# FFN projections as three 256-column matmuls per weight tile, with the two parts of their inputs in separate blocks

## The chip, the cores and the metric

The kernel runs on one core of a Trainium2 chip. The metric is the device time of one execution in microseconds. The engines are TensorE (PE; its weight loads are PEld), VectorE (DVE), ScalarE (ACT), GpSimd (POOL) and SyncE (SP). On-chip memory (SBUF) has 128 partitions; addresses below are bytes within a partition. Matmuls write to banks of PSUM.

## The reference

The input is a sequence of 256 tokens of width 1024, in float32. Two layers follow each other; a layer is

```
x = x + 0.5 * swiglu_ffn(rms_norm(x, ffn1_norm), gate_up, down)
x = x + mixer(rms_norm(x, mix_norm))       # layer 0: convolutions; layer 1: dilated attention
x = x + 0.5 * swiglu_ffn(rms_norm(x, ffn2_norm), gate_up, down)
```

where `swiglu_ffn(x) = (silu(gate) * up) @ w_down` with `gate, up = split(x @ w_gate_up)` and a hidden width of 2816. A last RMS norm ends it. There are therefore four FFN stages (two in each layer), and each multiplies 256 tokens by 1024 x 5632 and by 2816 x 1024 weights.

## The kernel before

Activations lie transposed: 128 features on the partitions, 256 tokens along the row. All weights come as one stream of "units" of 128 x 2048 floats (1 MB), which is 16 weight tiles of 128 x 128; SyncE's queue loads them in order into four `raw` buffers. For most units ScalarE then makes a rounded copy `w1` in the format fp32r (L126) and VectorE the remainder `w2 = raw - w1` (L127); `advance` (L130) issues loads and splits a few units ahead of their use. The unit buffers lie at multiples of 1024 bytes, so a weight tile of 512 bytes starts at 0 or at 512 modulo 1024.

Activations are split into two parts in the same way: the first part rounded, the second the remainder (`split_to`, L183). A product is then w1 x first + w1 x second + w2 x first; w2 x second is left out. There are two ways to write it:

- `mm3` (L158): three matmuls of 256 columns for a weight tile, L162 with w1 and the first part, L163 with w1 and the second, L164 with w2 and the first, all into the same 256 columns of PSUM.
- `mm2` (L166): two matmuls, L168 with w1 and both parts side by side as 512 columns, L169 with w2 and the first part as 256 columns. It leaves two halves in PSUM that are yet to be added.

An FFN stage (`ffn`, L364) has 22 projection steps of one unit each: a gate block and an up block of 128 features, 8 tiles each. With `project` (L314, mm3) gate and up fill one PSUM bank; with `project2` (L324, mm2) they fill two, and `join` (L334) adds the halves: a ScalarE copy (L338), a VectorE add (L339) for each, then a multiply by the norm's factor r (L340). Behind it come silu (L385), the product (L387) and the split into `gs` (L186, L187). `ONES` and `ONE_END` say which steps use mm3: the first 4, 0, 0 and 2 of the four stages, and the last one. Then come 8 output blocks of 22 tiles each (11 units): mm2 for seven of them, mm3 for the last, each added into x at L404 (once for each PSUM half). The mixers use mm3 (and plain fp32 matmuls, L160, for some units), but for the queries and keys of the attention, which use `project2`.

Each FFN or mixer reads its input from `xs`, which `Norm.add` (L287) fills block by block as the stage before it finishes. `xs` and `gs` hold, for each block of 128 features, the first part (1024 bytes) and behind it the second. Where they start is set by `XS_START` and `GS_START`; the tile `xs` itself is at a multiple of 1024, and the tile `gs` lies at 256 modulo 1024 in the first three stages and at 320 in the last.

TensorE executes its instructions in program order; the framework orders them by the program and its priorities, so that the first steps of a stage may stand among the last matmuls of the stage before.

Of the kernel before, what the change touches and what calls it, by code (L numbers as in the profile page):

```python
# [11 lines left out]
F32R = mybir.dt.float32r  # L12
# [5 lines left out]
P = 128  # L18
D = 1024
S = 256  # L20
DEPTH = 2
FF = 2816
ND = D // P
NF = FF // P
# [27 lines left out]
ONES = [4, 0, 0, 2]  # L52
ONE_END = 1
PRIO_F = 0
FFN_STEP = 40
# [4 lines left out]
WIDEC = 0  # L60
LINE = 1024
BASE = 16512
XS_START = {"F1": (288, 32), "MX": (192, 256), "F2": (288, 32)}
GS_START = (800, 800, 800, 736)
GROUPS = ((0, 2), (2, 4), (4, 6), (6, 8))
M_POOL = [0, 0, 0, 0]
B_POOL = [0, 0]
# [10 lines left out]
C_F1, C_MX, C_F2, C_FN = 0, DEPTH * ND, 2 * DEPTH * ND, 3 * DEPTH * ND  # L78
# [15 lines left out]
def trunk(ctx: ExitStack, tc: tile.TileContext, xin, wst, cst, bia, idn, out):  # L94
    nc = tc.nc
    keep = ctx.enter_context(tc.tile_pool(name="keep", bufs=1))
# [12 lines left out]
    at = {"load": 0, "split": 0}  # L109
# [20 lines left out]
    def advance(u, ahead_split=ahead_split):  # L130
        while at["load"] < min(n_units, u + ahead_load):
            load(at["load"])
            at["load"] += 1
        while at["split"] < min(n_units, u + ahead_split):
            split(at["split"])
            at["split"] += 1
# [3 lines left out]
    whole = {0} | {first_conv + i for i in WHOLE}  # L140

    class Stream:
        def __init__(self, u):
            self.u = u
# [8 lines left out]
    def take(n):  # L153
        st = Stream(used[0])
        used[0] += n
        return st

    def mm3(o, a, b, start, stop, check=False):  # L158
        if len(a) == 1:
            nc.tensor.matmul(o, a[0], b[-1], start=start, stop=stop, skip_group_check=check)  # L160
            return
        nc.tensor.matmul(o, a[0], b[0], start=start, stop=False, skip_group_check=check)  # L162
        nc.tensor.matmul(o, a[0], b[1], start=False, stop=False, skip_group_check=check)  # L163
        nc.tensor.matmul(o, a[1], b[0], start=False, stop=stop, skip_group_check=check)  # L164

    def mm2(o, w, b, start, stop):  # L166

        nc.tensor.matmul(o, w[0], b, start=start, stop=False, skip_group_check=True)  # L168
        nc.tensor.matmul(o[:, 0], w[1], b[:, 0], start=False, stop=stop, skip_group_check=True)  # L169


    x = keep.tile([P, ND, S], F32, name="x")
    xs_all = keep.tile([P, ND * 2 * S + LINE // 4], F32R, name="xs")
    const_all = keep.tile([P, LINE // 4], F32, name="const")
    const = const_all[:, :NCONST]
    ident = keep.tile([P, P], F32, name="ident")
# [6 lines left out]
    def split_to(o1, o2, src, scale=None):  # L183

        if scale is None:
            nc.scalar.copy(o1, src)  # L186
            nc.vector.tensor_sub(o2, src, o1.bitcast(F32))  # L187
        else:
            nc.scalar.activation(o1, src, AF.Copy, scale=scale)  # L189
            nc.vector.scalar_tensor_tensor(o2, src, scale, o1.bitcast(F32),  # L190
                                           op0=ALU.mult, op1=ALU.subtract)
# [86 lines left out]
    class Norm:  # L278


        def __init__(self, col, whole=None, start=0):
            self.col, self.whole = col, whole
            self.xs = xs_all[:, start // 4:start // 4 + ND * 2 * S].rearrange(
                "p (d t s) -> p d t s", d=ND, t=2)
            self.sums = tmp.tile([P, S], F32, name="sums")

        def add(self, d):  # L287
# [23 lines left out]
    def twice(r):  # L311
        return r[:, None, :].to_broadcast([P, 2, S])

    def project(st, base, xs, xg=None):  # L314

        bank = psa.tile([P, 2, S], F32, name="pa")
        for i in range(2):
            for k in range(ND):
                w = st.tile(base + 2 * k + i)
                b = (xs[:, k, 0], xs[:, k, 1]) if len(w) == 2 else (xg[:, k],)  # L320
                mm3(bank[:, i], w, b, k == 0, k == ND - 1)
        return bank

    def project2(st, base, xs):  # L324

        banks = []
        for i in range(2):
            bank = psa.tile([P, 2, S], F32, name="pa")
            for k in range(ND):
                mm2(bank, st.tile(base + 2 * k + i), xs[:, k], k == 0, k == ND - 1)  # L330
            banks.append(bank)
        return banks

    def join(v, banks, r):  # L334

        for i, bank in enumerate(banks):
            h = tmp.tile([P, S], F32, name="sq")
            nc.scalar.copy(h, bank[:, 1])  # L338
            nc.vector.tensor_add(v[:, i], bank[:, 0], h)  # L339
        nc.vector.tensor_mul(v, v, twice(r))  # L340
# [23 lines left out]
    def ffn(norm, after, between=None, first=None):  # L364
        _, r = norm.end(True, first is None)
        with tc.tile_pool(name="gp", bufs=1, reuse_waits="tile") as gp:
            st = take(NF)
            start = GS_START[st.u // FFN_STEP] // 4
            gs = gp.tile([P, NF * 2 * S + start], F32R, name="gs")[:, start:].rearrange(
                "p (f t s) -> p f t s", f=NF, t=2)  # L370
            for p in range(NF):
                advance(st.u + p)
                one = p < ONES[st.u // FFN_STEP] or p >= NF - ONE_END
                if one:
                    bank = first if first and p == 0 else project(st, p * UT, norm.xs)
                else:
                    banks = project2(st, p * UT, norm.xs)
                with tc.high_priority(offset=PRIO_F):
                    v = tmp.tile([P, 2, S], F32, name="v")
                    if one:  # L380
                        nc.vector.tensor_mul(v, bank, twice(r))
                    else:
                        join(v, banks, r)
                    sl = tmp.tile([P, S], F32, name="sl")
                    nc.scalar.activation(sl, v[:, 0], AF.Silu)  # L385
                    g = tmp.tile([P, S], F32, name="g")
                    nc.vector.tensor_mul(g, sl, v[:, 1])  # L387
                    split_to(gs[:, p, 0], gs[:, p, 1], g)
            if between:
                between(gs[:, NF - 1, 0, :1].bitcast(F32))  # L390
            st = take(NF * ND // UT)
            for d in range(ND):
                acc = psb.tile([P, 2, S], F32, name="pb")
                two = d < ND - 1
                for f in range(NF):
                    t = d * NF + f
                    if t % UT == 0 or f == 0:
                        advance(st.u + t // UT)
                    if two:
                        mm2(acc, st.tile(t), gs[:, f], f == 0, f == NF - 1)  # L400
                    else:
                        mm3(acc[:, 0], st.tile(t), (gs[:, f, 0], gs[:, f, 1]), f == 0, f == NF - 1)
                for i in range(2 if two else 1):
                    nc.vector.scalar_tensor_tensor(x[:, d], acc[:, i], 0.5, x[:, d],  # L404
                                                   op0=ALU.mult, op1=ALU.add)
                after.add(d)

    def out_half(st, accs, half, o, ds, ahead=(ahead_split,) * 2):

        for d in ds:  # L410
            for k in range(4):
                t = half * 32 + d * 4 + k
                if t % UT == 0:
                    advance(st.u + t // UT, ahead[t // UT % 2])
                mm3(accs[d // 2][:, d % 2], st.tile(t), [a[:, k] for a in o],
                    half == 0 and k == 0 and d % 2 == 0, half == 1 and k == 3, True)
# [290 lines left out]
    cold = psb.tile([P, P], F32, name="pb")  # L707
    for _ in range(WARM):
        nc.tensor.matmul(cold, ones, ones, start=True, stop=True)
    norm = Norm(C_F1, start=XS_START["F1"][0])  # L710
    for layer in range(DEPTH):
        nxt = Norm(C_MX + layer * ND, start=XS_START["MX"][layer])
        if layer == 0:
            ffn_first(norm, nxt)
        else:
            ffn(norm, nxt)
        norm, nxt = nxt, Norm(C_F2 + layer * ND, start=XS_START["F2"][layer])
        (conv if layer % 2 == 0 else attention)(norm, nxt)
        if layer < DEPTH - 1:
            norm, nxt = nxt, Norm(C_F1 + (layer + 1) * ND, start=XS_START["F1"][layer + 1])  # L720
            ffn(norm, nxt)
            norm = nxt
    with tc.tile_pool(name="fp", bufs=1, reuse_waits="tile") as fp:
# [7 lines left out]
        for i, (lo, hi) in enumerate(GROUPS):  # L731
            n = hi - lo
# [93 lines left out]
```

## Time and profile before

| | |
|---|---|
| time, median of 2 runs | 960.42 us (959.98 to 960.87) |
| the profiled execution's own time | 960.66 us |
| its span, first to last instruction | 958.9 us |
| PE busy | 945.5 us (99%), 5828 matmuls |
| weight loads busy | 845.8 us, 5828 loads |
| VectorE busy | 724.3 us (76%) |
| ScalarE busy | 543.3 us (57%) |
| granted clock of TensorE, mean | 0.997 |
| memory traffic | 176.24 MB, 184 GB/s |

A share of busy time is the union of an engine's instructions. Matmuls overlap in the pipeline, so the step of a stream of them is read from the starts, and not from the length of one.

### The profile page before, as it was taken

Reading aid. Unit: us, or ns where it says so; the run is one execution under the profiler, and the core shown is the slowest. Engines: PE = TensorE matmul, PEld = TensorE weight load, DVE = VectorE, ACT = ScalarE, POOL = GpSimd, SP = SyncE. Lnnn points to the kernel's source line nnn. Section 1 sums busy time; section 2 is a strip of 40 time slices with the busy share of each in tenths; the row PEclk is TensorE's granted clock in tenths of the full one; section 3 lists DMA queues with packets and bytes.
Section 4 is the critical chain, followed back from the end, with each engine's and each line's share of the span. In section 5 each row is a group of like instructions: output and inputs, shape, how many; then the busy total and the mean of one; then the engine's idle time right before and its main releaser. Section 6 shows DMA issues by size and latency. Waiting matters only on the chain.

```text
span 958.9 us, 15090 instructions
## 1 busy us (share of the span) xinstructions
PE 945.5 (99%) x5828; PEld 845.8 (88%) x5828; DVE 724.3 (76%) x1373; ACT 543.3 (57%) x975; POOL 47.1 (5%) x61
## 2 busy tenths in 40 slices
PE   8999999999999999999999999999999999999996
PEld 7988898999888888988988889898888998889886
DVE  7988866688879878766788877665698798788552
ACT  6666554488265565554466565444676565665541
POOL 0000000049600000000000000000000000000000
PEclk9999999999999999999999999999999999999998
DMA  8855555544176555555455555555553455555501
GB/s 328 291 205 192 178 206 189 178 159 148 45 260 213 193 207 181 180 211 181 176 194 202 176 191 205 178 195 212 195 191 129 149 186 194 194 202 177 194 26 44
DMA packets 27287, 176.24 MB, mean 184 GB/s; under 512 B 3024, under 2 KB 3792, under 8 KB 6864
## 3 DMA queue, kind: packets, MB, share of 16 engines
q1 hardware_dynamic: 26784, 174.67, 51.7%
q8 instruction: 45, 0.74, 0.3%
q10 hardware_dynamic: 432, 0.63, 0.2%
q14 instruction: 26, 0.21, 0.1%
HBM read 174.23 MB, written 1.05 MB: 183 GB/s over the span
## 4 chain that ended last, share of the span: by engine, by line
PE 90%; POOL 3%; DVE 3%; ACT 1%; DMA 1%; issue 1%; SPq 0%; DVEq 0%; POOLq 0%; ACTq 0%
PE pa L168 33%; PE pa L169 17%; PE pb L168 15%; PE pb L169 8%; PE pa L162 4%; PE pa L163 3%; PE pa L164 3%; POOL yp L486 3%; PE pa L160 2%; PE pb L162 1%; PE pb L163 1%; PE pb L164 1%; DVE pb L463 1%; PE pa L352 1%; PE pb L652 1%
## 5 line engine op out<-in xcount | busy, mean ns | idle before, releaser
L127 DVE TENSOR_TENSOR w<-raw,w 128x1024 fp32r<-128x1024 f32 (+1 forms) x316 | 377.0, 1205 | 136.3 <-ACT w L126 135.9
L168 PE MATMUL pa<-xs,w 128*128 128x512 f32 x1376 | 479.4, 391 | 0.1
L126 ACT CAST w<-raw 128x1024 fp32r<-128x1024 f32 (+1 forms) x316 | 320.5, 1032 | 133.5 <-PE pa L168 49.7
L169 PE MATMUL pa<-xs,w 128*128 128x256 f32 x1376 | 387.2, 282 | 0.0
L168 PEld LDWEIGHTS pa<-xs,w 128*128 128x128 f32 x1376 | 258.1, 188 | 54.9 <-DVE xs L190 0.7
L169 PEld LDWEIGHTS pa<-xs,w 128*128 128x128 f32 x1376 | 260.0, 189 | 0.3
L168 PE MATMUL pb<-gs,w 128*128 128x512 f32 x616 | 213.7, 390 | 0.0
L169 PE MATMUL pb<-gs,w 128*128 128x256 f32 x616 | 173.7, 282 | 0.0
L168 PEld LDWEIGHTS pb<-gs,w 128*128 128x128 f32 x616 | 115.6, 188 | 24.1
L169 PEld LDWEIGHTS pb<-gs,w 128*128 128x128 f32 x616 | 116.4, 189 | 0.0
L385 ACT ACTIVATE sl<-v 128x256 f32<-128x256 f32 x88 | 36.8, 418 | 108.7 <-DVE v L340 104.3
L338 ACT COPY sq<-pa 128x256 f32<-128x256 f32 x172 | 62.9, 366 | 28.6 <-PE pa L169 26.1
L163 PE MATMUL pa<-xs,w 128*128 128x256 f32 x272 | 76.3, 281 | 0.1
L162 PE MATMUL pa<-xs,w 128*128 128x256 f32 x272 | 76.3, 282 | 0.0
L164 PE MATMUL pa<-xs,w 128*128 128x256 f32 x272 | 76.2, 281 | 0.0
L339 DVE TENSOR_TENSOR v<-pa,sq 128x256 f32<-128x256 f32 x156 | 65.5, 420 | 0.0
L404 DVE SCALAR_TENSOR_TENSOR x<-pb,x 128x256 f32<-128x256 f32 x60 | 25.4, 423 | 42.5 <-PE pb L169 28.5
L189 ACT ACTIVATE xs<-x,const 128x256 fp32r<-128x256 f32 x48 | 24.3, 506 | 55.2 <-DVE x L404 43.1
L486 POOL TENSOR_TENSOR yp<-yp,prod 128x256 f32<-128x256 f32 x55 | 45.1, 822 | 208.8 <-ACT prod L485 204.8
L340 DVE TENSOR_TENSOR v<-v,rr 128x512 f32<-128x512 f32 x78 | 53.6, 688 | 0.0
L162 PEld LDWEIGHTS pa<-xs,w 128*128 128x128 f32 x272 | 51.4, 190 | 0.3
L163 PEld LDWEIGHTS pa<-xs,w 128*128 128x128 f32 x272 | 51.1, 188 | 0.5 <-DVE xs L190 0.3
(155 smaller groups left out, 900.7 us busy)
## 6 DMA issues: line engine op xcount, KB each, us to landing
raw<-wst SPq DMA_DIRECT2D x159, 1024.0 KB, 4.8
bt<-bia SPq DMA_DIRECT2D x8, 384.0 KB, 3.3
raw<-wst SPq DMA_DIRECT2D x7, 256.0 KB, 6.3
raw<-wst SPq DMA_DIRECT2D x2, 512.0 KB, 5.6
x<-xin SPq DMA_DIRECT2D x3, 256.0 KB, 5.7
out<-y SPq DMA_DIRECT2D x2, 256.0 KB, 2.5
out<-y ACTq DMA_DIRECT2D x2, 256.0 KB, 2.4
x<-xin SPq DMA_DIRECT2D x2, 128.0 KB, 3.2
```

Of the source, the lines that this page charges most:

```text
L126: nc.scalar.copy(w1[u][:, c], raw[u][:, c])
L127: nc.vector.tensor_sub(w2[u][:, c], raw[u][:, c], w1[u][:, c].bitcast(F32))
L162: nc.tensor.matmul(o, a[0], b[0], start=start, stop=False, skip_group_check=check)
L163: nc.tensor.matmul(o, a[0], b[1], start=False, stop=False, skip_group_check=check)
L164: nc.tensor.matmul(o, a[1], b[0], start=False, stop=stop, skip_group_check=check)
L168: nc.tensor.matmul(o, w[0], b, start=start, stop=False, skip_group_check=True)
L169: nc.tensor.matmul(o[:, 0], w[1], b[:, 0], start=False, stop=stop, skip_group_check=True)
L338: nc.scalar.copy(h, bank[:, 1])
L339: nc.vector.tensor_add(v[:, i], bank[:, 0], h)
L340: nc.vector.tensor_mul(v, v, twice(r))
L385: nc.scalar.activation(sl, v[:, 0], AF.Silu)
L486: nc.gpsimd.tensor_add(yp[:, c], yp[:, c], t)
```

## The change

All FFN tiles are multiplied with `mm3`. The new function `blocks` lays the inputs out as two blocks: all first parts together, and all second parts together behind them, each block with a start of its own modulo 1024 bytes. `XS_AT` and `GS_AT` give these two starts for each stage, `GS_BASE` the place modulo 1024 that the tile `gs` itself has. For the mixers' inputs (`MX`) both starts stay what they were, 192 and 256. The tile `xs` grows by 2048 bytes.

```
-XS_START = {"F1": (288, 32), "MX": (192, 256), "F2": (288, 32)}
-GS_START = (800, 800, 800, 736)
+XS_AT = {'F1': ((192, 256), (128, 128)), 'MX': ((192, 192), (256, 256)), 'F2': ((192, 320), (448, 448))}
+GS_AT = ((192, 448), (64, 128), (320, 320), (384, 384))
+GS_BASE = (256, 256, 256, 320)
+THREE = (0, 1, 2, 3)
...
+    def blocks(t, base, at, n):
+        lo = (at[0] - base) % LINE
+        step = n * S * 4 + (at[1] - at[0]) % LINE
+        a = t[:, lo // 4:(lo + 2 * step) // 4].rearrange("p (t q) -> p t q", t=2)
+        return a[:, :, :n * S].rearrange("p t (k s) -> p k t s", k=n)
...
-    xs_all = keep.tile([P, ND * 2 * S + LINE // 4], F32R, name="xs")
+    xs_all = keep.tile([P, ND * 2 * S + 3 * LINE // 4], F32R, name="xs")
...
-        def __init__(self, col, whole=None, start=0):
+        def __init__(self, col, whole=None, at=(0, 0)):
             self.col, self.whole = col, whole
-            self.xs = xs_all[:, start // 4:start // 4 + ND * 2 * S].rearrange(
-                "p (d t s) -> p d t s", d=ND, t=2)
+            self.xs = blocks(xs_all, 0, at, ND)
...
-            start = GS_START[st.u // FFN_STEP] // 4
-            gs = gp.tile([P, NF * 2 * S + start], F32R, name="gs")[:, start:].rearrange(
-                "p (f t s) -> p f t s", f=NF, t=2)
+            n = st.u // FFN_STEP
+            gs = blocks(gp.tile([P, NF * 2 * S + 3 * LINE // 4], F32R, name="gs"), GS_BASE[n],
+                        GS_AT[n], NF)
             for p in range(NF):
                 advance(st.u + p)
-                one = p < ONES[st.u // FFN_STEP] or p >= NF - ONE_END
+                one = n in THREE or p < ONES[n] or p >= NF - ONE_END
...
-                two = d < ND - 1
+                two = d < ND - 1 and n not in THREE
...
-    norm = Norm(C_F1, start=XS_START["F1"][0])
+    norm = Norm(C_F1, at=XS_AT["F1"][0])
```

The other calls of `Norm` take `at=XS_AT[...]` in the same way.

## Rows read from the trace of the kernel before

**Rows 1.** The page: span, and busy time, share and instructions of each engine.
```profile
span 958.9 us, 15090 instructions
...
PE 945.5 (99%) x5828; PEld 845.8 (88%) x5828; DVE 724.3 (76%) x1373; ACT 543.3 (57%) x975; POOL 47.1 (5%) x61
```

**Rows 2.** The page: the chain of work that ended last, by engine.
```profile
PE 90%; POOL 3%; DVE 3%; ACT 1%; DMA 1%; issue 1%; SPq 0%; DVEq 0%; POOLq 0%; ACTq 0%
```

**Rows 3.** Two stretches: length, busy PE, PEld, DVE, ACT, POOL; PEclk, DMA share, GB/s.
```profile
31.40:125.60 94.20, 94.20 (x545) 83.51 (x544) 78.91 (x126) 58.72 (x105) 0.00 (x0) 1.00 0.60 212
...
131.30:184.60 53.30, 53.30 (x309) 47.25 (x308) 34.42 (x48) 25.71 (x35) 0.00 (x0) 1.00 0.54 196
```

**Rows 4.** Waits of PE, the longest: total us, times, longest us.
```profile
PE pa L352 <- DVE xg L348: 1.9, 1, 1.9
```

**Rows 5.** Timeline of PE (start, length): first and last L168 of two stretches.
```profile
31.43 0.40 PE L168 MATMUL pa<-xs,w 128*128 128x512 f32 x1
...
125.39 0.39 PE L168 MATMUL pa<-xs,w 128*128 128x512 f32 x1
...
131.33 0.39 PE L168 MATMUL pb<-gs,w 128*128 128x512 f32 x1
...
184.37 0.39 PE L168 MATMUL pb<-gs,w 128*128 128x512 f32 x1
```

**Rows 6.** Timeline of PE: first and last tile of one output block.
```profile
184.72 0.28 PE L162 MATMUL pb<-gs,w 128*128 128x256 f32 x1
...
192.07 0.28 PE L162 MATMUL pb<-gs,w 128*128 128x256 f32 x1
```

**Rows 7.** Groups of PE by line: count, busy us, mean ns, idle before.
```profile
L168 PE MATMUL pa<-xs,w 128*128 128x512 f32 x1376 | 479.4, 391 | 0.1
...
L168 PE MATMUL pb<-gs,w 128*128 128x512 f32 x616 | 213.7, 390 | 0.0
...
L162 PE MATMUL pa<-xs,w 128*128 128x256 f32 x272 | 76.3, 282 | 0.0
...
L162 PE MATMUL pb<-gs,w 128*128 128x256 f32 x88 | 24.5, 279 | 0.0
```

**Rows 8.** Timeline of PE in the convolution's input projection: start, and later.
```profile
192.89 0.28 PE L163 MATMUL pa<-xs,w 128*128 128x256 f32 x1
...
194.59 0.28 PE L163 MATMUL pa<-xs,w 128*128 128x256 f32 x1
...
227.33 0.28 PE L163 MATMUL pa<-xs,w 128*128 128x256 f32 x1
...
231.92 0.28 PE L163 MATMUL pa<-xs,w 128*128 128x256 f32 x1
```

**Rows 9.** Timeline of PE in the attention's output projection.
```profile
750.90 0.28 PE L162 MATMUL pa<-o,w 128*128 128x256 f32 x1
...
752.70 0.28 PE L162 MATMUL pa<-o,w 128*128 128x256 f32 x1
```

**Rows 10.** fp32 matmuls of 256 columns: a run of 13 (timeline), their mean (groups).
```profile
277.84 2.97 PE L160 MATMUL pa<-ob,raw 128*128 128x256 f32 x13
...
L160 PE MATMUL pa<-ob,raw 128*128 128x256 f32 x64 | 14.2, 381 | 0.0
```

**Rows 11.** Groups of VectorE and ScalarE around the join, the splits and x.
```profile
L127 DVE TENSOR_TENSOR w<-raw,w 128x1024 fp32r<-128x1024 f32 x304 | 368.4, 1223 | 133.6 <-ACT w L126 133.2
L339 DVE TENSOR_TENSOR v<-pa,sq 128x256 f32<-128x256 f32 x156 | 65.5, 420 | 0.0
...
L404 DVE SCALAR_TENSOR_TENSOR x<-pb,x 128x256 f32<-128x256 f32 x60 | 25.4, 423 | 42.5 <-PE pb L169 28.5 <-PE pb L164 12.7
...
L338 ACT COPY sq<-pa 128x256 f32<-128x256 f32 x172 | 62.9, 366 | 28.6 <-PE pa L169 26.1 <-DVE sq L187 1.1 <-DVE v L339 1.1
```

**Rows 12.** Timeline of PE in a query and key projection of the attention.
```profile
694.73 0.40 PE L168 MATMUL pa<-xs,w 128*128 128x512 f32 x1
...
699.58 0.40 PE L168 MATMUL pa<-xs,w 128*128 128x512 f32 x1
```

More of the change, by code (lines that the diff above doesn't have):

```diff
@@ L709, in trunk @@
         nc.tensor.matmul(cold, ones, ones, start=True, stop=True)
-    norm = Norm(C_F1, start=XS_START["F1"][0])
+    norm = Norm(C_F1, at=XS_AT["F1"][0])
     for layer in range(DEPTH):
-        nxt = Norm(C_MX + layer * ND, start=XS_START["MX"][layer])
+        nxt = Norm(C_MX + layer * ND, at=XS_AT["MX"][layer])
         if layer == 0:
@@ L716, in trunk @@
             ffn(norm, nxt)
-        norm, nxt = nxt, Norm(C_F2 + layer * ND, start=XS_START["F2"][layer])
+        norm, nxt = nxt, Norm(C_F2 + layer * ND, at=XS_AT["F2"][layer])
         (conv if layer % 2 == 0 else attention)(norm, nxt)
         if layer < DEPTH - 1:
-            norm, nxt = nxt, Norm(C_F1 + (layer + 1) * ND, start=XS_START["F1"][layer + 1])
+            norm, nxt = nxt, Norm(C_F1 + (layer + 1) * ND, at=XS_AT["F1"][layer + 1])
             ffn(norm, nxt)
```

## Prediction

> **What bounds the kernel now.** I read the page first. TensorE (PE) is busy for 945.5 of a span of 958.9 us [rows 1], and the chain of work that ended last runs through PE for 90% of the span [rows 2]. Busy is not yet "at its peak", so the next view is the table by stage: in a projection stretch and in a down stretch PE is busy for the whole of the stretch at a granted clock of 1.00, which is the 2.4 GHz level, with weights arriving at 212 and 196 GB/s [rows 3]. The list of waits says the same from the other side: the longest wait of PE anywhere is 1.9 us, at the very start [rows 4]. So inside the feed-forward (FFN) stages the time is the number of weight tiles times the step from one tile to the next on PE, and nothing else.
>
> The step is read from the timeline, first start to last start over the count, because a matmul's own length (282 or 390 ns) overlaps its neighbours'. A two-matmul tile (L168 with 512 columns, then L169 with 256): in a down stretch 154 L168 start from 131.33 to 184.37 us, 153 steps of 346.7 ns; in a projection stretch 272 start from 31.43 to 125.39, 271 steps of 346.7 ns [rows 5]. A three-matmul tile (L162 to L164, 256 columns each): the last output block of the same down stage goes from 184.72 to 192.07 in 21 tiles, 350.0 ns each, 116.67 per matmul [rows 6]. 768 columns at 2.4 GHz would be 320 ns for either form, so both carry 27 to 30 ns a tile that isn't columns.
>
> **The change, part by part.** *Matmuls.* L168 ran 1376 times on xs, of which 128 belong to the attention's queries and keys (8 pairs of 16 tiles) and stay; 616 times on gs [rows 7]. So 1248 + 616 = 1864 tiles go from two matmuls to three: 1864 more matmuls and 1864 more weight loads. At the step of [rows 6], which is the one for the *old* places, that is 1864 x (350.0 - 346.7) = **+6.2 us**, all on the path, since PE has no slack there.
>
> *Places.* This is the unknown. Today both parts of every FFN input start at 32 modulo 256 bytes (288 and 32 for xs; for gs 256 + 800 or 320 + 736, which is 32 modulo 1024); weight tiles start at 0 or 512. The new places are all multiples of 64: modulo 256, xs (192, 0), (192, 64), (128, 128), (192, 192) and gs (192, 192), (64, 128), (64, 64), (128, 128) for the four stages in order. Tiles added or grown are whole multiples of 1024, so nothing else moves within its 1024. What does the trace say of the step at other places? The three-matmul form also runs in the mixers, with the same weights. The convolution has both parts at 192: at its start 5 tiles take 192.89 to 194.59, 340.0 ns each, **113.33** per matmul; later, behind a stall, 13 tiles take 227.33 to 231.92, 353.1 ns, **117.7** [rows 8]. The attention's output projection reads its input at 0 modulo 256: 5 tiles from 750.90 to 752.70, 360.0 ns, **120.0** [rows 9]. So the same instruction costs from 113.3 to 120.0, by its place and by how the stream was entered. Above, 120.0 is the bound. Below, a bound from another form: 13 fp32 matmuls of 256 columns take 2.97 us, less the last one's 0.38 from issue to end, so 215.8 ns a step, 2.5 over twice 106.7 (256 columns at 2.4 GHz) [rows 10]; with the same 2.5 a 256-column fp32r step would be 109.2.
>
> After the change 1864 + 232 tiles of the FFN are three-matmul tiles (the 232: 144 on xs, that is 272 less the convolution's 128, and 88 on gs [rows 7]), 6288 matmuls, so each ns of step is worth 6.3 us: time = 960.66 + 6.2 + 6.288 x (step - 116.67). It gives 919.9 at 109.2, 945.9 at 113.33, 966.9 at 116.67, 973 at 117.7 and 987.8 at 120.0.
>
> I take **114.0**: the new places are on the grid of the convolution's 192, whose stream entered without a stall stood at 113.33, the nearest row; some of the eight stretches will fall into a slower rhythm, as the convolution did, and 80% at 113.33 with 20% at 116.67 makes 114.0. Then 960.66 + 6.2 - 6.288 x 2.67 = **950.1**.
>
> A rule of the Trainium skill speaks against any gain by place. By "TensorE: Matmul & The Clock Gate" (Step-by-step: what each phase is for), the moving operand and the weight load have two independent SBUF read ports, so that a load takes nothing from a running matmul; by it, places would change nothing and the change would only add. The trace disagrees: four steps for one shape, as above.
>
> *Joining the halves.* For 78 pairs of banks the join goes: 156 adds of 420 ns and the same number of 366 ns copies, and the multiply by r now reads PSUM; seven of eight output blocks also lose one of two 423 ns additions into x [rows 11]. All of it lies beside PE, which waits for none of it, so I cost it at nothing; VectorE and ScalarE get freer, not later. The same cover is what would hide it if the step fell: a weight unit of 16 tiles at 109.2 x 48 = 5.2 us still needs only two splits of 1.22 us on VectorE [rows 11] and 1 MB from memory, 200 GB/s where 212 is already seen [rows 3].
>
> *One PSUM bank instead of two per projected block.* PE can run further ahead at a stage's start. The stalls there are single ones within the 13.4 us that PE idles in all [rows 1]; taken at zero, ends -1.5 and +1 us (its longest wait is 1.9 [rows 4]).
>
> *Two blocks.* The attention's 512-column matmul now reads two runs 8 KB apart instead of 1 KB, at an unchanged place. Steady, its tile takes 694.73 to 699.58 in 14 steps, 346.4 ns [rows 12], the same as in the FFN. Taken at zero; if the jump cost as much as a third matmul, 128 x 3.3 ns = 0.4 us.
>
> The profiled execution took 960.66 us, 1.8 us around its span, and is 0.2 us above the median of 960.42, so the sum stands for the median too.
>
> **Rivals.** *Places don't matter* (the rule above): every stretch stays at 116.67 as [rows 6], **967 us**. For it: places 288 and 32 don't differ now, and two-matmul tiles are 346.7 in both kinds of stretch. Against it: [rows 8, 9]. Chance 0.15.
>
> *Conflict-free places*: the load and the moving read no longer meet, the step falls below 112.6, towards 109.2: **920 to 941 us**, faster by over 2%. For it: the fp32 step shows that 2.5 ns of extra is possible [rows 10], and separate places for the two parts give each matmul of the three its own offset against the weights. Against it: no fp32r row is steady below 113.3. Chance 0.33.
>
> *Worse places*: at 0 modulo 256 the three-matmul step is 120.0; the second part of stage 1's xs is put there, and if 64 and 128 behave like 0 rather than like 192, all is at 120.0: **988 us**. It decides from a mean step of 118.7 on (979.6 us). Against it: only one place of sixteen is 0, and it is read by one matmul of three in one stage's projections. Chance 0.08. Between the two, at the convolution's later 117.7, stands 973 us, chance 0.06.
>
> That the change would miss its places is excluded by the sizes above.
>
> **The numbers.** My forecast, a mean step from 112.6 to 116.0 (941 to 963 us), has 0.38. With 2% (19 us, about what a measurement here can tell from no change) the borders are 941.2 and 979.6: faster 0.33, same 0.38 + 0.15 + 0.06 = 0.59, slower 0.08. The range goes from near the conflict-free end, 922, to 971, which leaves out about 0.07 below (steps under 109.5) and 0.12 above. The forecast's own range is 941 to 963.
>
> **What would show it.** No L168 on gs and 128 on xs left; L162 1248 + 144 + 128 = 1520 on xs and 704 on gs. First start to last start in each of the eight stretches gives its step: about 340 ns a tile where I am right, 350 where places don't matter, 328 where conflicts go. A step that differs between stretches at equal places would say that the entry, not the place, sets it. I am wrong if PE shows idle time inside a stretch, since then a supplier and not the step would bound.

## The result, and the profile after

The changed kernel takes 977.94 us (median of 2 runs, 977.34 to 978.55) against 960.42: 1.0173 times the time before, interval 1.0150 to 1.0196. That is slower by 1.7%, outside the range of 922 to 971 us. The profiled execution took 978.55 us.

The page of the changed kernel: span, busy time of the engines, chain by engine, and groups of instructions, as in [rows 1, 2, 7, 11].

```profile
span 976.8 us, 18444 instructions
...
PE 961.9 (98%) x7692; PEld 936.0 (96%) x7692; DVE 661.0 (68%) x1189; ACT 493.6 (51%) x819; POOL 47.2 (5%) x61
...
PE 91%; POOL 3%; DVE 3%; DMA 1%; ACT 1%; issue 0%; SPq 0%; DVEq 0%; POOLq 0%; ACTq 0%
...
L172 PE MATMUL pa<-xs,w 128*128 128x256 f32 x1520 | 426.2, 281 | 0.0
...
L172 PE MATMUL pb<-gs,w 128*128 128x256 f32 x704 | 197.4, 280 | 0.0
L390 DVE TENSOR_TENSOR v<-pa,rr 128x512 f32<-128x512 f32 x88 | 60.7, 690 | 117.9 <-PE pa L174 117.8
```

The counts are those that the prediction named, 1520 and 704, and 1864 matmuls were added in all. VectorE lost 63 us of work and ScalarE 50; the chain still runs through PE. The next view is the stretches, with the columns of [rows 3]: the start in two pieces, then a projection and a down stretch of stage 1.

```profile
8.00:9.40 1.40, 0.00 (x0) 0.00 (x0) 0.97 (x3) 0.74 (x3) 0.00 (x0) 0.70 0.95 304
9.40:14.00 4.60, 4.57 (x11) 3.66 (x12) 3.67 (x12) 3.32 (x9) 0.00 (x0) 0.50 1.05 385
...
20.00:136.00 116.00, 116.00 (x987) 116.00 (x986) 86.54 (x122) 59.07 (x86) 0.00 (x0) 1.00 0.62 218
...
136.60:198.60 62.00, 62.00 (x529) 62.00 (x528) 35.24 (x45) 28.21 (x38) 0.00 (x0) 1.00 0.54 187
```

Inside the FFN stretches PE is busy for every microsecond at a clock of 1.00, as before, so nothing supplies it too late and the step is still the whole of the time there. Its size stands in PE's timeline of the changed kernel (start, length): the start of the program, then the first and last tile of the down stretches of stages 1 and 4, 175 steps each.

```profile
9.43 8.36 PE L361 MATMUL pa<-xg,raw 128*128 128x256 f32 x24 [2.87 <-DMA raw<-wst]
...
17.44 0.47 PE L172 MATMUL pa<-xs,w 128*128 128x256 f32 x1
...
136.59 0.28 PE L172 MATMUL pb<-gs,w 128*128 128x256 f32 x1
...
198.43 0.28 PE L172 MATMUL pb<-gs,w 128*128 128x256 f32 x1
...
903.53 0.28 PE L172 MATMUL pb<-gs,w 128*128 128x256 f32 x1
...
965.83 0.28 PE L172 MATMUL pb<-gs,w 128*128 128x256 f32 x1
```

(198.43 - 136.59) / 175 = 353.4 ns a tile, and (965.83 - 903.53) / 175 = 356.0, where the forecast needed some 342. The start is 3.6 us late as well; the same rows of the kernel before:

```profile
8.62 5.57 PE L352 MATMUL pa<-xg,raw 128*128 128x256 f32 x24 [1.91 <-DVE xg L348]
13.85 0.47 PE L162 MATMUL pa<-xs,w 128*128 128x256 f32 x1
```

The same 12 fp32 matmuls (24 rows, for the trace shows each as two) took 5.57 us before and 8.36 after. The stretches of both timelines, first tile to last, account for the whole difference:

| stretch | before, us | after, us | more |
|---|---|---|---|
| the first FFN tile starts at | 13.85 | 17.44 | 3.59 |
| stage 1: projections, down | 117.14, 60.74 | 118.80, 61.83 | 1.66, 1.09 |
| stage 2 with the convolution: projections, down | 214.41, 60.74 | 216.43, 61.84 | 2.02, 1.10 |
| stage 3: projections, down | 122.28, 60.74 | 125.51, 61.84 | 3.23, 1.10 |
| attention (to the start of stage 4) | 115.70 | 115.65 | -0.05 |
| stage 4: projections, down | 119.64, 60.74 | 121.70, 62.30 | 2.06, 1.56 |
| from the last down tile to the end of the span | 10.49 | 10.97 | 0.48 |

The sum is 17.84, and the spans differ by 17.9 us: 13.8 in the FFN stretches, 3.6 at the start.

### The profile page after: what moved, and what is told of

It is laid out like the page before. It is cut to its first block, busy times and chain, and to the rows that moved or that the text cites. A ratio compares the mean times of both kernels' runs of the same rounds, so it can differ in the third digit from the quotient of the medians.

```text
span 976.8 us, 18444 instructions
## 1 busy us (share of the span) xinstructions
PE 961.9 (98%) x7692; PEld 936.0 (96%) x7692; DVE 661.0 (68%) x1189; ACT 493.6 (51%) x819; POOL 47.2 (5%) x61
## 4 chain that ended last, share of the span: by engine, by line
PE 91%; POOL 3%; DVE 3%; DMA 1%; ACT 1%; issue 0%; SPq 0%; DVEq 0%; POOLq 0%; ACTq 0%
PE pa L173 19%; PE pa L172 18%; PE pa L174 18%; PE pb L172 9%; PE pb L173 9%; PE pb L174 8%; POOL yp L495 3%; PE pa L178 3%; PE pa L170 2%; PE pa L179 2%; DMA raw<-wst 1%; PE pa L361 1%; DVE pb L472 1%; PE pb L661 1%; ACT w L128 0%
## 5 line engine op out<-in xcount | busy, mean ns | idle before, releaser
L173 PE MATMUL pa<-xs,w 128*128 128x256 f32 x1520 | 428.0, 282 | 0.2
L172 PE MATMUL pa<-xs,w 128*128 128x256 f32 x1520 | 426.2, 281 | 0.0
L174 PE MATMUL pa<-xs,w 128*128 128x256 f32 x1520 | 425.9, 280 | 0.0
L174 PEld LDWEIGHTS pa<-xs,w 128*128 128x128 f32 x1520 | 287.1, 189 | 0.0
L173 PEld LDWEIGHTS pa<-xs,w 128*128 128x128 f32 x1520 | 286.1, 188 | 0.9 <-DVE xs L200 0.8
L172 PEld LDWEIGHTS pa<-xs,w 128*128 128x128 f32 x1520 | 286.4, 189 | 0.2
L174 PE MATMUL pb<-gs,w 128*128 128x256 f32 x704 | 197.7, 281 | 0.0
L172 PE MATMUL pb<-gs,w 128*128 128x256 f32 x704 | 197.4, 280 | 0.0
L173 PE MATMUL pb<-gs,w 128*128 128x256 f32 x704 | 197.4, 280 | 0.0
L390 DVE TENSOR_TENSOR v<-pa,rr 128x512 f32<-128x512 f32 x88 | 60.7, 690 | 117.9 <-PE pa L174 117.8
L174 PEld LDWEIGHTS pb<-gs,w 128*128 128x128 f32 x704 | 132.9, 189 | 0.0
L172 PEld LDWEIGHTS pb<-gs,w 128*128 128x128 f32 x704 | 132.6, 188 | 0.0
L173 PEld LDWEIGHTS pb<-gs,w 128*128 128x128 f32 x704 | 132.1, 188 | 0.0
L196 ACT CAST gs<-g 128x256 fp32r<-128x256 f32 x88 | 35.7, 407 | 33.8 <-DVE g L396 33.6
L178 PE MATMUL pa<-xs,w 128*128 128x512 f32 x128 | 45.7, 400 | 0.0
L413 DVE SCALAR_TENSOR_TENSOR x<-pb,x 128x256 f32<-128x256 f32 x32 | 13.5, 422 | 45.8 <-PE pb L174 45.8
L396 DVE TENSOR_TENSOR g<-sl,v 128x256 f32<-128x256 f32 x88 | 36.7, 418 | 0.0
```

## The experiments

Two theories stood at the beginning. *Place*: the step belongs to the addresses of the input (and of the weights), so each place has its price. *Entry*: an address allows several steps, and how the stream was entered picks one. Places are given modulo 64 bytes from here on, where 288 is 32 and all places of the change are 0; that nothing beyond this remainder counts is an assumption, which no run tested by itself. Each number of the table is from PE's timeline of that run's profiled execution: last start less first over the number of steps, 240 for a projection stretch and 153 for a down stretch. F1 holds the places of the stages 1 and 3, F2 those of 2 and 4; semicolons part the stages, each with its projections and its down stretch where two places are given.

| ns per tile | stage 1 | stage 2 | stage 3 | stage 4 |
|---|---|---|---|---|
| before (two matmuls; 32) | 346.7, 346.7 | 346.7, 346.7 | 346.7, 346.7 | 346.7, 346.7 |
| after (0) | 353.3, 353.3 | 353.3, 353.4 | 356.0, 353.4 | 353.3, 356.0 |
| e1 (32) | 350.0, 350.0 | 350.0, 350.0 | 350.0, 350.0 | 350.0, 350.0 |
| e2 (two matmuls; 0, 32, 0, 32) | 346.7, 353.3 | 346.7, 346.7 | 351.1, 348.8 | 346.7, 346.7 |
| e3 (16, 8; 48, 24; 40, 56; 4, 36) | 350.0, 353.2 | 355.0, 360.0 | 357.5, 354.0 | 370.0, 363.2 |
| e4 (parts at unequal places) | 353.3, 353.3 | 351.1, 353.3 | 353.3, 353.3 | 350.0, 355.6 |
| e5 (two matmuls; mostly unequal) | 346.7, 346.6 | 346.7, 356.6 | 346.7, 357.2 | 350.0, 371.7 |
| e6 (32, 0; 0, 32; 16, 48; 32, 0; weights at 32) | 360.0, 355.0 | 355.0, 359.9 | 351.4, 340.1 | 360.0, 355.0 |
| e8 (the change, with filling matmuls at the start) | 353.3, 340.1 | 353.3, 353.4 | 356.0, 353.4 | 353.3, 360.0 |
| e9 (the change again) | 357.8, 340.0 | 353.3, 353.4 | 356.0, 353.3 | 353.3, 360.0 |
| e13 (all at 0) | 353.3, 353.3 | 340.0, 340.0 | 353.3, 353.3 | 353.3, 353.3 |
| e14 (all at 16) | 350.0, 350.0 | 350.0, 350.0 | 356.0, 356.0 | 350.0, 350.0 |
| e15 (all at 16, entered twice) | 350.0, 340.0 | 350.0, 340.0 | 350.0, 340.0 | 350.0, 340.0 |
| e16 (all at 16, projections entered twice) | 340.0, 340.0 | 356.0, 356.0 | 340.0, 340.0 | 340.0, 340.0 |

First number: projections; second: down (of e15 without the step that holds the small matmul, which makes its mean 340.6). The means of e5's stages 3 and 4 begin with a disturbed block, of which more below.

**Form and places taken apart.** Three matmuls at the old places:

```
XS_AT F1 ((288, 288), (32, 32)), F2 the same;  GS_AT ((32, 32),) * 4
```

> The change with both parts of every FFN input back at 32 modulo 64 bytes (288 and 32 for xs, 32 for gs), still in two blocks and still three matmuls a tile. Theory A (the place modulo 64 sets the three-matmul step: 350.0 ns a tile at 32, 353.3 at 0): all eight stretches at 350.0, time 966 to 968 us plus whatever the start of the program costs (up to 3.6 us, as in the changed kernel), so about 967 to 971. Theory B (the way a stream is entered sets the step, places do nothing): stretches at 353 as in the changed kernel, 977 us.

Measured: 350.0 in all eight stretches, 969.76 us (967.82 to 971.0), ratio 1.0085 (1.0068 to 1.0101). Its timeline, first and last tile of the down stretch of stage 1:

```profile
133.88 0.28 PE L172 MATMUL pb<-gs,w 128*128 128x256 f32 x1
...
195.13 0.28 PE L172 MATMUL pb<-gs,w 128*128 128x256 f32 x1
```

61.25 / 175 = 350.0. The form's own price is the 3.3 ns a tile of the prediction, 6.2 us of the 8.8 that e1 loses against the 960.98 of the kernel before on that chip; its profiled execution also started the FFN 2.0 us late (15.84 against 13.85). The change lost 17.5 us, so about half of its loss comes with the places.

Two matmuls at places like the change's, and three at eight places never used:

```
e2: THREE = ();  XS_AT F1 ((192, 256), (128, 128)), F2 ((288, 288), (32, 32))
    GS_AT ((192, 448), (32, 32), (320, 320), (32, 32))
e3: XS_AT F1 ((16, 16), (40, 40)), F2 ((48, 48), (4, 4));  GS_AT ((8, 8), (24, 24), (56, 56), (36, 36))
```

> Two matmuls a tile again, as before the change (first steps and last ones with three as before), but in two blocks; the places are the new ones in the first FFN of each layer and its hidden values, the old ones (32 modulo 64) in the second FFN of each layer. Theory A: two-matmul stretches at the new places above 346.7 ns a tile (350 or more), those at the old places 346.7; about 962 us. Theory B: 346.7 in all, 960 us. If the two blocks alone cost something, the stretches at the old places show it.

> Three matmuls a tile; both parts at the same place, another one in each of the eight stretches. Modulo 64, in the order of the stretches: 16, 8, 48, 24, 40, 56, 4, 36. Theory A: steps differ by place, between 340 and 360 ns a tile, and not with the order of the stretches. Theory B: 350 to 354 in all of them without order. A stretch below 346.7 would be a place at which three matmuls beat two.

Measured: e2 963.98 us; at 32 (stages 2 and 4) every stretch stays at 346.7, at 0 (stages 1 and 3) they stand from 346.7 to 353.3, so the two-matmul form depends on the place too. e3 985.82 us, with steps from 350.0 to 370.0. The timelines, first and last L178 or L172 of a down stretch (153 and 175 steps); first e2, stage 1:

```profile
131.59 0.40 PE L178 MATMUL pb<-gs,w 128*128 128x512 f32 x1
...
185.65 0.40 PE L178 MATMUL pb<-gs,w 128*128 128x512 f32 x1
```

then e3, stage 2, at 24:

```profile
413.62 0.28 PE L172 MATMUL pb<-gs,w 128*128 128x256 f32 x1
...
476.62 0.28 PE L172 MATMUL pb<-gs,w 128*128 128x256 f32 x1
```

54.06 / 153 = 353.3 and 63.00 / 175 = 360.0. One instruction with one shape takes 350.0 to 370.0 ns a tile in eight stretches that differ in their places, where e1 at one place had 350.0 in all eight. Entry could still make some of that difference; e10 below takes the two apart, and there "places don't matter" falls for good.

**Is it the distance between input and weights?** Unequal parts in both forms, then the weights moved by 32 bytes:

```
e4: XS_AT F1 ((32, 0), (16, 48)), F2 ((0, 32), (48, 16));  GS_AT ((32, 64), (64, 32), (16, 32), (32, 16))
e5: THREE = ();  XS_AT F1 ((16, 16), (16, 48)), F2 ((32, 0), (48, 0));  GS_AT ((48, 48), (0, 32), (16, 32), (16, 0))
e6: a pad of 32 bytes ahead of the weight tiles, GS_BASE + 32
    XS_AT F1 ((32, 32), (16, 16)), F2 ((0, 0), (32, 32));  GS_AT ((0, 0), (32, 32), (48, 48), (0, 0))
```

> Three matmuls a tile; the two parts at different places. Modulo 64, (first, second) in the order of the stretches: (32, 0), (32, 0), (0, 32), (0, 32), (16, 48), (16, 32), (48, 16), (32, 16). Theory A with the first part alone deciding: the first two stretches at 350, the third and fourth at 353. With every matmul having the step of its own part: 351 and 352. A third theory, that parts at different places avoid each other's conflicts: below 346.7.

> Two matmuls a tile (three in the steps that had three before), in two blocks, at other places. Modulo 64, (first, second) in the order of the eight stretches: (16, 16), (48, 48), (32, 0), (0, 32), (16, 48), (16, 32), (48, 0), (16, 0). The two-matmul run so far stood at 346.7 ns a tile at (32, 32) and at (0, 0) in one stretch, at 353.3, 351 and 349 in other stretches at (0, 0). If the place sets the step, the eight differ by place between 340 and 360; the theory that 346.7 is a floor of this form has none below it.

> The changed kernel with the split weights w1 and w2 moved by 32 bytes. Places of the inputs modulo 64, both parts, in the order of the stretches: 32, 0, 0, 32, 16, 48, 32, 0. If only the distance between input and weights counts, inputs at 32 now behave as those at 0 did (353.3 ns a tile, or 340), inputs at 0 as those at 32 did (350.0), 16 as 48 did (355) and 48 as 16 did (350). If the input's own place counts, 32 stays at 350.0, 0 at 353.3, 16 at 350.0, 48 at 355. If neither, all are alike.

Measured: e4 972.88 us, all stretches from 350.0 to 355.6: unequal parts give no gain.

e5: 978.9 us; equal parts stay at 346.7, unequal ones stand from 346.7 to 356.6 (stage 2, down). Its down stretches of stages 3 and 4 began behind a wait of some 3.3 us for the split of the gate, and its time contains the waits. In stage 4 the granted clock was 0.50 behind the wait, for most of the first block; in stage 3 it stayed at 1.00. From the second output block to the seventh the steps were 356.7 in stage 3 (parts at 16 and 32) and 353.3 in stage 4 (16 and 0), and these, not the 357.2 and 371.7 of the table, belong to the places.

e6: 979.54 us; with the weights at 32, an input at 32 costs 360.0, at 0 355.0, at 16 351.4 and at 48 340.1. Had the input's address alone decided, 32 would have stayed at 350.0. Had the distance between input and weights alone decided, 32 would be like 0 with weights at 0 and 48 like 16, which fits one of the steps seen there (360.0, 340.0), but 0 would be like 32 (350.0) and 16 like 48 (355.0), which doesn't fit. So both addresses matter, and neither rule does. That the two reads meet in memory is argued from this, and not shown.

**The start.**

```
e8:  if k == 3:  for _ in range(8): matmul(cold, ones, ones)     # behind the fourth of the first step's eight blocks
e9:  no edit
```

> The changed kernel with 8 more matmuls of ones, 128 columns each, put between the fourth and the fifth block of the first unit, where PE waits 2.9 us for weights at 1.00 of the clock and then runs 24 matmuls at 0.50. Theory: the clock fell in that wait; with the wait filled it stays at 1.00, the first three-matmul tile starts at about 14 us as in the kernel before (17.4 in the changed one), and the time falls by 2 to 3.6 us against the changed kernel run beside it, to 974 to 976. Rival: the start is late because its weights land later, and the clock is not the cause: 17 us and 977 to 978.

> The changed kernel once more, as it is, beside the one with the filled wait: 977 to 978.5 us if its slow start belongs to it, and now and then about 974.5 if the start varies from one execution to the next, as three matmuls at the old places did (967.8 to 971.0).

Measured: e8 976.69 us (975.51 to 978.45), ratio 1.0161. The clock stayed at 1.00, but the filling missed the wait: PE's wait lies between the second and the third block (1.70 us here), and of the eight matmuls one ran ahead of it and seven behind the fourth block, from 10.26 us on. In e9 the clock stayed at 1.00 behind a wait of 1.27 us without any filling, and the first FFN tile came at 14.05, not at e8's 15.98. So e8 doesn't show whether filling the wait would keep the clock.

e9: 976.55 us (975.74 to 978.21), ratio 1.016 (1.0144 to 1.0176). The same program started well this time; its windows (columns as above) of the start and of the convolution:

```profile
9.40:14.00 4.60, 4.26 (x20) 3.47 (x19) 4.03 (x13) 3.69 (x10) 0.00 (x0) 1.00 1.06 371
250.00:300.00 50.00, 46.95 (x251) 41.35 (x250) 38.88 (x109) 21.85 (x40) 8.07 (x11) 0.97 0.53 190
```

and its timeline:

```profile
14.05 0.47 PE L172 MATMUL pa<-xs,w 128*128 128x256 f32 x1
...
135.22 0.28 PE L172 MATMUL pb<-gs,w 128*128 128x256 f32 x1
...
194.73 0.28 PE L172 MATMUL pb<-gs,w 128*128 128x256 f32 x1
```

The start is at 14.05 and not 17.44, so a late start isn't in every execution of the change; this one lost 2.1 us in stage 2 instead, where PE waited 2.8 us for the convolution (1.7 in the other) and the clock fell to 0.97 on the mean. More important is the down stretch: 59.51 / 175 = **340.0**, where the same program with the same addresses stood at 353.4. The place theory in its plain form has fallen: a place allows a set of steps. (This may have been another chip than the result's; but in e16 below twelve executions of one program on one chip spread from 951 to 965 us, two of them at 951.04 and 962.42 with mean granted clocks of 0.996 and 0.997.)

**What picks the step.** A matmul of two columns of ones is put before every projection step and every output block, which breaks the stream and starts it again. By the place theory nothing but its own time should be added; by the entry theory the steps behind it change:

```
e10: matmul(bank[:, 1, :2], ones, ones[:, :2])  in project, and in each output block
     places 0 in stage 1, 32 in stage 2, 16 in stage 3, 48 in stage 4
```

> Three matmuls a tile with one small matmul (2 columns of ones) put ahead of every projection step and every output block, so that the stream is entered afresh 22 and 8 times in a stage. Places modulo 64: stage 1 the changed kernel's (0), stage 2 all at 32, stage 3 all at 16, stage 4 all at 48. If the entry sets the rhythm, steps and blocks of one stretch differ among themselves, by whole steps such as 340, 350, 353 and 360 ns a tile. If the place alone sets it, all blocks of a stretch are alike: 353 in stage 1, 350 in stage 2, 350 in stage 3, 355 in stage 4. The small matmuls add some 0.1 us each, 120 of them: about 985 us.

Measured: 996.61 us, which holds the price of 129 small matmuls (some 0.22 us each; 10 of them in the convolution's projection, which uses `project` too). PE's timeline, those of four steps in a row in stage 3:

```profile
507.70 0.28 PE L326 MATMUL pa<-ones 128*128 128x2 f32 x2
...
513.53 0.28 PE L326 MATMUL pa<-ones 128*128 128x2 f32 x2
...
519.19 0.28 PE L326 MATMUL pa<-ones 128*128 128x2 f32 x2
...
525.12 0.28 PE L326 MATMUL pa<-ones 128*128 128x2 f32 x2
```

The distances are 5.83, 5.66 and 5.93 us: 16 tiles of 350.0, 340.0 and 356.2 ns and 0.22. In the projections at 16 the steps come round in this order with every small matmul, but of the output blocks there the first two stand at 350.0 and 340.0 and the other six all at 356.0. At 0 the steps turn between 353.0 and 357.8 in the projections and, from the second output block on, stay at 340.0. At 32 the projections and output blocks stand at 350.0 but for one projection step of 353.3, and at 48 all stand at 355.0, however often the stream is entered (e3's stretch at 48, in stage 2 and not in stage 4, stood at 355.0 as well). So the place sets which steps there are, and where there are several, re-entry changes between them.

**Using it.** All places at 0 and at 16, without and with small matmuls in chosen steps `p` of a projection and output blocks `d`:

```
e13: all places (192, 192)                e12: + small matmul at p in (2, 3), d in (0, 1)
e14: all places (16, 16), at p == 3       e15: + at d == 0
```

> The same places without the small matmuls. If the entry alone decides, the stretches fall to 340, 353.3 or 360 as they come in, the first ones of the stages like the changed kernel's (353.3): 965 to 978 us. If (192, 192) is a better place by itself, most of them are at 340 and the time is below 955 us.

> Three matmuls a tile, all inputs with both parts at 192 (0 modulo 64), the place at which a freshly entered stream stood at 340.0 ns a tile in 13 of 14 blocks. One small matmul ahead of the third and fourth projection step and of the first and second output block of each stage, 16 in all at about 0.22 us. If such an entry brings and keeps the 340.0 rhythm, the stretches stand at 340 behind it: 960.9 - 1864 x 6.7 ns - 232 x 10 ns + 3.6 = 950 us, faster than the kernel before by 1.1%. If the rhythm falls back or the entry is chance: some stretches at 353 to 360, 955 to 980 us.

> Three matmuls a tile, all inputs at 16 modulo 64, one small matmul ahead of the fourth projection step of each stage. At this place the re-entered stream went through 350.0, 340.0 and 356.2 ns a tile in turn, one step on with each small matmul. If the stream comes in at 350 and one small matmul moves it to 340, and the output blocks take over the rhythm: 340 from the fourth step to the end of all four stages, about 949 us. If the entry falls elsewhere: 350 or 356, 967 to 980 us.

> The same with a second small matmul ahead of the first output block of each stage. If the rhythm moves on with each one, as it did, the output blocks stand one further on in the turn 350, 340, 356 than the projections before them: where the projections are at 340 the output blocks are at 356.2, where they are at 350 the output blocks are at 340. If the rhythm is not carried from a stretch to the next, the two kernels' output blocks show no such order.

Measured: e13 970.77 us (968.28 to 975.93), ratio 1.0093 (1.0060 to 1.0127). Where projections and down have the same place, the down stretch keeps the step of the projections in all four stages: the stream carries it.

e12: 965.07 (962.74 to 972.66), ratio 1.0044 (1.0018 to 1.0071), where 950 was expected: 340 in the blocks of stages 1 and 2, but 353 in those of stages 3 and 4, which the small matmuls there didn't move.

e14: 972.43 (970.65 to 974.02), ratio 1.0117 (1.0100 to 1.0135): carried again, at 350.0 or 356.0. The hoped-for 340 was missed because the small matmul found the stream at 350.0 in the stages 1, 2 and 4 and left it there, where e10's had moved 350.0 to 340.0; in stage 3 it moved 340.0 to 356.0.

e15: 967.05 (965.22 to 969.94), ratio 1.0072 (1.0052 to 1.0092): one small matmul ahead of the output blocks turns 350.0 to 340.0 in all four stages. Its timeline in stage 1: the last 17 tiles of the projections (the first and the last of them), the small matmul, then the first and the last tile of the down stretch.

```profile
128.82 0.28 PE L172 MATMUL pa<-xs,w 128*128 128x256 f32 x1
...
134.42 0.28 PE L172 MATMUL pa<-xs,w 128*128 128x256 f32 x1
...
134.77 0.28 PE L407 MATMUL pb<-ones 128*128 128x2 f32 x2
...
134.91 0.36 PE L172 MATMUL pb<-gs,w 128*128 128x256 f32 x1
...
194.50 0.28 PE L172 MATMUL pb<-gs,w 128*128 128x256 f32 x1
```

5.60 / 16 = 350.0 before it; 59.59 / 175 = 340.5 behind it, 340.0 without the first, longer step. Where a place allows several steps, entry decides, and it can be moved on purpose, though not every time (e12, e14).

Three matmuls in the down projections alone, and two small matmuls in the projections at 16:

```
e11: THREE = (), two = False;  XS_AT at 32 as before;  GS_AT ((192, 192), (16, 16), (0, 0), (48, 48))
e16: all places (16, 16), small matmul at p in (3, 4)
```

> Projections as in the kernel before (two matmuls a tile at 32 modulo 64, three in the first and last steps), all output blocks with three matmuls, hidden values at 0, 16, 0 and 48 modulo 64, both parts alike. If a stretch falls into the 340.0 ns rhythm it gains 154 x 6.7 + 22 x 10 = 1.2 us against the kernel before; at 353.3 it loses 1.1 us, at 360 2.3 us. All four at 340: 956 us; all at 353: 965 us; the entry deciding by chance, 958 to 966 us.

> As e14, with small matmuls ahead of the fourth and of the fifth projection step of each stage and none ahead of the output blocks. In e15 all four projections stood at 350.0 behind the first small matmul, and the next one, ahead of the output blocks, brought all four output stretches to 340.0. If a small matmul moves the rhythm on and the stream carries it, the second one here brings the projections to 340.0 from their fifth step on, and the output blocks take it over: seven or eight of eight stretches at 340, about 952 us, faster than the kernel before by 0.9%. If the rhythm falls by chance, stretches between 340 and 356, 962 to 972 us.

Measured: e11 965.19 us (964.51 to 965.74), ratio 1.0038 (1.0026 to 1.0051), with 340.1, 356.0, 360.0 and 355.0 ns in the four down stretches. Over 154 tiles each that is -1.0, +1.4, +2.0 and +1.3 us against 346.7, in sum +3.7; measured 4.0 over the 961.19 of the kernel before on that chip. The timeline of e11's stage 3:

```profile
591.80 0.28 PE L172 MATMUL pb<-gs,w 128*128 128x256 f32 x1
...
654.79 0.28 PE L172 MATMUL pb<-gs,w 128*128 128x256 f32 x1
```

62.99 / 175 = 359.9 at 0, where e9 had 340.0 in stage 1 at places that are the same modulo 64 (0 and 0 here, 192 and 448 there).

e16: **957.39 us** (951.04 to 965.36, 12 runs) against 961.06, ratio 0.9947 (0.9926 to 0.9968), the only version under the kernel before, by about half a percent. The expected 952 us were reached by three of the twelve executions (951.04 to 952.78). Its timeline: one step of the projections between two small matmuls, the next step, and the down stretches of stages 1 and 2.

```profile
27.84 0.28 PE L172 MATMUL pa<-xs,w 128*128 128x256 f32 x1
...
32.74 0.28 PE L172 MATMUL pa<-xs,w 128*128 128x256 f32 x1
33.09 0.28 PE L327 MATMUL pa<-ones 128*128 128x2 f32 x2
...
33.65 0.28 PE L172 MATMUL pa<-xs,w 128*128 128x256 f32 x1
...
38.41 0.28 PE L172 MATMUL pa<-xs,w 128*128 128x256 f32 x1
...
131.23 0.28 PE L172 MATMUL pb<-gs,w 128*128 128x256 f32 x1
...
190.73 0.28 PE L172 MATMUL pb<-gs,w 128*128 128x256 f32 x1
...
410.40 0.28 PE L172 MATMUL pb<-gs,w 128*128 128x256 f32 x1
...
472.70 0.28 PE L172 MATMUL pb<-gs,w 128*128 128x256 f32 x1
```

4.90 us for 14 tiles, 350.0 ns, before the small matmul, and 4.76 for 14, 340.0, behind it; 340.0 still holds 100 us later in the down stretch. Stage 2 was entered at another point of the turn and stood at 356.0. The profiled execution took 961.38 us. With its stage 2 at 340.0 too, from the fifth step on, (288 + 176) tiles x 16 ns would be another 7.4 us; that is an estimate, no run had it in its profile.

## Why the prediction was wrong, point by point

- **What bounds it: right.** PE is busy for the whole of every FFN stretch. The joins that went, 63 us of VectorE and 50 of ScalarE, bought no time, as "I cost it at nothing" said.
- **The matmuls, +6.2 us: right.** e1, the change at the old places, shows 350.0 in all eight stretches.
- **The places: wrong, and this step failed**: "I take 114.0: the new places are on the grid of the convolution's 192, whose stream entered without a stall stood at 113.33, the nearest row", with 80% at 113.33 and 20% at 116.67. Weighted by their tiles the eight stretches stand at 354.0 ns, 118.0 per matmul. No stretch stood at 340.0 and none at 350.0. In the prediction's own formula, 960.66 + 6.2 + 6.288 x (118.0 - 116.67) = 975.2 us.
  The row was read rightly and meant less than I took from it. [rows 8] showed 340.0 and 353.1 at one place in one stage, so it already said that the place doesn't fix the step. I took the faster as the rule and the slower as its disturbance. e9, e13 and e15 show that they are two members of one set, of which entry picks one; 353.3 is as steady as 340.0, and the change fell on it six times of eight.
- **The rivals.** *Places don't matter* is refuted by e1 and e10: 350.0 at 32 and 355.0 at 48 through all entries but one, and 340.0 to 357.8 at 0. By the Trainium skill, "TensorE: Matmul & The Clock Gate" (Step-by-step: what each phase is for), the moving operand and the weight load read through independent ports. What the prediction drew from that, that places change nothing, doesn't hold here: the same tile took 340.0 to 370.0 ns. Whether the two reads do meet isn't shown. *Conflict-free*, to which I gave 0.33, was seen in none of the runs: no stretch of three matmuls was under 340.0 ns. Its 2.5 ns of extra came from steps of 215.8 ns and weren't met on steps of half that length. *Worse places*, 120.0 a matmul, exist at the change's own places: in e9, the same program, the down stretch of stage 4 stands at 360.0. It is one stretch of eight and not all. The nearest was the case of 0.06, "at the convolution's later 117.7, stands 973 us".
- **The start: no term in the sum.** PE waited 2.87 us for weights, and the fp32 matmuls behind it ran at a granted clock of 0.50, the 1.2 GHz level, where those of the kernel before ran at 1.00. That makes 3.6 us here: these matmuls began 0.8 us later and took 2.8 us more. The length of the first wait doesn't settle it alone: the clock held behind 0.90 to 1.96 us in before, e2, e4, e6, e8, e9 and e10, but also behind 2.78 us in e11, and it was lost behind 1.89 to 4.08 us in after, e1, e3, e5 and e12 to e16. Nor is it luck alone, as far as the mean granted clock tells: it was 0.994 in four of the change's six executions (the result's two and e9's four), and 0.994 or less in only four of the 62 of the kernel before that ran beside the experiments. So the changed kernel seems to lose the clock more often; why is open.
- **One PSUM bank, two blocks: within their ends.** 975.2 with 3.6 for the start would be 978.8; 978.55 was measured. The FFN stretches grew by 13.8 us and not 14.6, and the end of the span by 0.5. The missing 0.7 us lie in stage 1 (some 0.35) and in stage 2 with the convolution (some 0.25). In stages 3 and 4 the projections take 0.5 to 0.6 us more than their steady steps add up to, in both kernels, so an earlier start of the stages (ends -1.5 and +1) doesn't show there; one bank for two wasn't tried by itself. The attention, which reads the two blocks, is the same to 0.05 us.

The sign was lost with the one choice: at 116.67 or above, every case that I named is slower than before.

What stays open: whether the address counts beyond its remainder modulo 64 (the change's 128 and 128 in stage 3 stood at 356.0 in after, e8 and e9 alike, while 192 and 192 showed only 340.0 and 353.3 in e11, e12 and e13); what sets the entry at a stage's start (e16's stage 2 differs from its stages 1, 3 and 4 with the same program), and how the addresses of input and weights make the set. A kernel that enters every stage at 340.0 wasn't found.

## What to carry to other kernels

When a trace shows two steady steps for one instruction at one address, carry both through the forecast as cases of their own; a short stretch at the faster one is no evidence for a long one. Where matmuls with a weight load each are the bound, read the step by first and last start in every stretch separately, and try the operands' places modulo 64 bytes and a tiny matmul between stretches before trading two long matmuls for three short ones. Where an unchanged program is timed, look at whether the clock held through its first wait before comparing less than 4 us.

## What the runs showed of the hardware

- The step of a three-matmul tile (256 columns each, a weight load each) takes steady values that depend on the start of its input. With the weight tiles at 0 modulo 64 bytes: 340.0, 353.3, 356.0, 357.8 or 360.0 at 0; 340.0, 350.0 or 356.0 at 16; 350.0 (353.3 once) at 32; 355.0 at 48; up to 370.0 at 4. With the weights 32 bytes on (e6): 360.0 at 32, 355.0 at 0.
- A step, once entered, holds over hundreds of tiles and, where both have the same address, over the change from projections to down (e13, e14). A matmul of two columns can move it, in e10's projections at 16 in the order 350.0, 340.0, 356.2; it left 350.0 as it was in three stages of e14, and 353.3 at 0 in the output blocks of stages 3 and 4 of e12.
- The two-matmul tile isn't exempt: 346.7 at 32, from 346.7 to 353.3 at 0 (e2), 356.6 with parts at 0 and 32 and 350.0 with parts at 48 and 0 (e5).
